# An encoder trunk on one core: activations stored by the parity of their tokens, and matmuls that read two runs in turn

## The chip, the core and the metric

The kernel runs on one core of one Trainium2 chip. The metric is device time in microseconds (us), the median of three runs. TensorE multiplies matrices: a block of 128 x 128 weights is loaded (the stationary operand), and then the columns of a moving operand are drawn through it and summed in PSUM. VectorE, ScalarE and the DMA queues prepare operands and take results away.

## What is computed

Two layers of an encoder on 256 tokens of width 2048. Each layer has a combined input projection, differential attention (8 heads) beside multi-head latent attention (8 heads), gated branches, an output projection, a SwiGLU block of width 5632, and a gated per-layer embedding:

```
h   = RMSNorm(x)
z   = h @ w_in[i]                  # diff q | k | v | q latent | kv latent | rope key | two gates
A   = differential attention;  B = multi-head latent attention
m   = sigmoid(gate_diff) * (A @ w_branch_diff) + sigmoid(gate_mla) * (B @ w_branch_mla)
x   = x + m @ w_out[i]
x   = x + SwiGLU(RMSNorm(x))
x   = x + sigmoid(RMSNorm(x) @ w_ple_gate) * (p[i] @ w_ple_in)
```

At the end stands one more RMSNorm. All inputs and outputs are float32. Attention is bidirectional, without a mask.

## The kernel before

Activations lie transposed: the 128 partitions hold features, the free dimension holds the 256 tokens (`T`). The stream `xT` has 16 such chunks. Every product keeps float32 accuracy by splitting both operands into a rounded part (`hi`, type float32r) and the remainder (`lo`), and summing three of the four partial products.

An operand tile is `[128, 512]`: columns 0 to 255 are `hi` of the 256 tokens, columns 256 to 511 are `lo`. The tiles `ua0` to `ua15` and `ub0` to `ub15` hold most operands; `fa`, `fb` and `fc` hold queries, keys and rotated queries. `split` fills a tile: ScalarE writes `hi` (L245, L246), VectorE the remainder (recorded under the helpers' lines L75 and L78).

The weights come by DMA in pieces of 512 KB (`piece`, tile `w`), and are split in the same way into `whi` (ScalarE, L182) and `wlo` (VectorE, L75).

`product` makes 128 output features for all tokens. For each of its chunks `emit` issues two matmuls:

- L212: weights `whi` against the whole operand tile, 512 columns (`hi` and `lo` side by side), into all 512 columns of an accumulator `mm`;
- L213: weights `wlo` against the `hi` half, 256 columns, into the second half of `mm`.

ScalarE and VectorE then add the two halves of `mm` (`joined`, or `accumulate` for the stream). The very last product of the program takes three matmuls of 256 columns instead (`whole`, L208 to L210).

`values` is the product with sides exchanged: the activations are stationary (128 tokens at a time), and the weights, 512 columns of `whi` or `wlo`, are the moving operand (L396 to L398). Its results `vals` have tokens in the partitions, as attention needs them. The host lays these weights out with `wide`, the others with `tiles`.

`scores` multiplies queries (stationary) by keys (moving, `three`). `turned` transposes the softmax weights on TensorE (L360), and the sums over keys follow (L568 for differential attention, L625 for latent attention). `norm` sums squares over partitions with a column of ones (L272), and `spread` turns the resulting two columns of 128 numbers into a row of 256 that stands in all partitions, with one matmul against a diagonal (L281). `rotated` exchanges halves of a head for the rotary embedding (L320). Those last ones, L568 too, are plain float32, which the program issues as two instructions each.

The order of instructions on each engine is set by a scheduler that simulates the program when it is built; DMA issues stand on SyncE's queue.

Of the kernel before, what the change touches and what calls it, by code (L numbers as in the profile page):

```python
# [19 lines left out]
P = 128  # L20
T = 256
# [32 lines left out]
def encoder(ctx, tc, x, p, positions, cols, lams, wq, wk, wv, wcq, wckv, wkr, wga, wgb,  # L54
            w_q_up, w_kn, w_v, w_bd, w_bm, w_out, w_gate, w_up, w_down, w_pin, w_pg, rope_c, out):
    nc = tc.nc
    V, A, PE = nc.vector, nc.scalar, nc.tensor
# [10 lines left out]
    def scratch(tag, bufs, n=T):  # L68
        return tmp.tile([P, n], F32, tag=tag, name=tag, bufs=bufs)

    def bank(ps=ps_at, tag="at", name="at", shape=(P, 2 * T)):
        return ps.tile(list(shape), F32, tag=tag, name=name)

    def tt(o, a, b, op):
        return V.tensor_tensor(out=o, in0=a, in1=b, op=op)  # L75

    def stt(o, a, s, b, op0, op1):
        return V.scalar_tensor_tensor(out=o, in0=a, scalar=s, in1=b, op0=op0, op1=op1)  # L78

    def ts(o, a, s1, s2, op0, op1=ALU.bypass):  # L80
        return V.tensor_scalar(out=o, in0=a, scalar1=s1, scalar2=s2, op0=op0, op1=op1)  # L81
# [10 lines left out]

    def operand(t):
        return t.rearrange("p c t -> p (c t)")


    xT = const.tile([P, NC, T], F32, name="xT")
# [15 lines left out]
    ones = const.tile([P, P], F32, name="ones")  # L113
# [81 lines left out]
    last_split, last_mm, chores, sq0, step = [], [], [], [], []  # L195
# [8 lines left out]
    def emit(acc, hi, lo, at, us, first, last, whole):  # L204
        for j, u in enumerate(us):
            s, start, stop = slice((at + j) * P, (at + j + 1) * P), first and j == 0, last and j == len(us) - 1
            if whole:
                PE.matmul(acc[:, :T], hi[:, s], u[:, :T], start=start, stop=False)  # L208
                PE.matmul(acc[:, :T], hi[:, s], u[:, T:], start=False, stop=False)
                PE.matmul(acc[:, :T], lo[:, s], u[:, :T], start=False, stop=stop)  # L210
            else:
                PE.matmul(acc, hi[:, s], u, start=start, stop=False)  # L212
                PE.matmul(acc[:, T:], lo[:, s], u[:, :T], start=False, stop=stop)  # L213

    def product(src, us, whole=False):

# [18 lines left out]
    def joined(acc, o=None):  # L235
        t = scratch("join", 3)
        A.activation(t, acc[:, T:], AF.Copy)  # L237
        o = scratch("a", 4) if o is None else o
        tt(o, acc[:, :T], t, ALU.add)
        return o  # L240

    def split(u, src, gain=None):
        hi, lo = u[:, :T], u[:, T:]
        if gain is None:
            return A.activation(hi, src, AF.Copy), tt(lo, src, hi.bitcast(F32), ALU.subtract)  # L245
        return A.activation(hi, src, AF.Copy, scale=gain), stt(lo, src, gain, hi.bitcast(F32), ALU.mult, ALU.subtract)  # L246

    def rsqrt(src, n, eps, width):

        v, y, a = (stat.tile([P, 2 * DH], F32, tag="r" + s, name="r" + s, bufs=2)[:, :width] for s in "vya")  # L250
        ts(v, src, 1.0 / n, eps, ALU.mult, ALU.add)
        ts(y.bitcast(I32), v.bitcast(I32), -0.5, 1597463007.0, ALU.mult, ALU.add)
        for _ in range(3):
            stt(a, y, -0.5, y, ALU.mult, ALU.mult)
            tt(a, a, v, ALU.mult)
            stt(y, a, 1.5, y, ALU.add, ALU.mult)
        return y
# [9 lines left out]
    def norm(sums, n):  # L267

        s = bank()
        for j, a in enumerate(sums):  # L270
            for b in range(2):
                PE.matmul(s[:, b : b + 1], a[:, b * P : (b + 1) * P], ones[:, 0:1], start=j + b == 0, stop=j + b == len(sums))  # L272
        return rsqrt(s[:, 0:2], n, EPS, 2)

    def spread(col, copied=True):

        dg = stat.tile([P, 2, P], F32, tag="dg", name="dg", bufs=1)
        for b in range(2):
            ts(dg[:, b, :], ident, col[:, b : b + 1], None, ALU.mult)
        s = bank()  # L280
        PE.matmul(s[:, :T], ones, dg, start=True, stop=True)  # L281
        if not copied:
            return s[:, :T]
        row = stat.tile([P, T], F32, tag="row", name="row", bufs=2)
        A.activation(row, s[:, :T], AF.Copy)  # L285
        return row
# [11 lines left out]
    def stream(us, gain):  # L298

        acc = squares()  # L300

        def add(c):
            split(us[c], xT[:, c, :], g(gain, c))
            square_into(acc, xT[:, c, :], c == 0)

        return acc, add
# [11 lines left out]
    def rotated(a, c_, s_, o=None):  # L318
        r = bank()
        PE.matmul(r[:, :T], swap, a, start=True, stop=True)  # L320
        t = scratch("sh", 2)
        tt(t, r[:, :T], s_, ALU.mult)
        tt(a, a, c_, ALU.mult)
        tt(a, a, t, ALU.add)
        if o is None:
            for j, t in enumerate(krs):
                split(t[64 * j : 64 * j + 64], a[64 * j : 64 * j + 64])
        else:
            split(o, a)

    def three(q, k):
        return [(q[:, :T], k[:, T:]), (q[:, T:], k[:, :T]), (q[:, :T], k[:, :T])]

    def scores(*maps):

# [41 lines left out]
    def values(src, us, load=None):  # L377

        vals = stat.tile([P, 2, 2, 512], F32, tag="vals", name="vals", bufs=1)
        n = len(us)  # L380
        order = [(half, a, 2) for half in range(2) for a in range(0, n, 2)]
        if load:
            order = [(half, a, 1) for a in range(BOTH) for half in range(2)] + [s for s in order if s[1] >= BOTH]
        banks = {}
        for half, a, m in order:
            if a == 0:
                banks[half] = [bank(ps_mm, "mm", "mmv") for _ in range(2)]
            if load and not half:
                load(a, m)
            hi, lo = piece(src[half][:, a * 512 : (a + m) * 512], 4 * m)  # L390
            for j in range(m):
                s = slice(j * 512, (j + 1) * 512)
                for b in range(2):
                    xh = us[a + j][:, b * P : (b + 1) * P]
                    xl = us[a + j][:, T + b * P : T + (b + 1) * P]
                    PE.matmul(banks[half][b], xh, hi[:, s], start=a + j == 0, stop=False)  # L396
                    PE.matmul(banks[half][b], xl, hi[:, s], start=False, stop=False)  # L397
                    last_mm[:] = [PE.matmul(banks[half][b], xh, lo[:, s], start=False, stop=a + j == n - 1)]  # L398
            if half or a + m < n:
                yield  # L400
            if a + m == n:
                for b in range(2):
                    A.activation(vals[:, b, half, :], banks[half][b], AF.Copy)
                if not half:
                    yield vals
# [15 lines left out]
    for L in range(DEPTH):  # L421
# [27 lines left out]


        qk = [(ub[h], operand(fa(h, F32R))) for h in range(DH)]

        def queries_keys(h):
            for which, w in enumerate((wq, wk)):
                a = joined(product(w[L, h], ua))
                sh = scratch("sh", 2)
                V.stream_shuffle(sh, a, ROPE16)
                tt(sh, sh, sr, ALU.mult)
                tt(a, a, cr, ALU.mult)
                tt(a, a, sh, ALU.add)  # L460
                split(qk[h][which], a)


        cq, ckv = ub[8:12], ub[12:14]
        qn, kn, qr = [], [], ub[14:]
# [19 lines left out]
        def queries_up(n):  # L485
            for acc in pair(w_q_up[L, n : n + 2], cq):
                if n < MH:
                    qn.append(operand(fa(len(qn), F32R)))
                    split(qn[-1], joined(acc))
                else:  # L490
                    if n > MH:
                        qr.append(operand(fc(len(qr) - 2, F32R)))
                    at = qr[len(qr) - 1] if n > MH else qr[ropes[0]]
                    rotated(joined(acc), cos_m, sin_m, at)
                    ropes[0] += 1
# [149 lines left out]
        acc, add = stream(ub, f"g_ffn{L}")  # L645
# [11 lines left out]
        for part, (f0, f1) in enumerate(FF_PARTS):  # L657
            for f in range(f0, f1):
                a = pre.pop(0) if pre else joined(product(w_gate[L, f], ub))
                tt(a, a, R, ALU.mult)  # L660
                s = scratch("sig", 2)
# [3 lines left out]
                b = pre.pop(0) if pre else joined(product(w_up[L, f], ub))  # L665
# [3 lines left out]
            if last:  # L669
                acc, add = stream(ub, f"g_ple{L}")  # L670
# [12 lines left out]
        if final:  # L683
            sums = [squares(), squares()]
# [5 lines left out]
        else:  # L690
            acc, add = stream(ua, f"g_mix{L + 1}")
        for n in range(NC):
            if final and n == NC - 1:
                a = scratch("a", 4)
                tt(a, product(w_pg[L, n], ub, True), R, ALU.mult)
            else:
                a = pre.pop(0) if pre else joined(product(w_pg[L, n], ub))
                tt(a, a, R, ALU.mult)
            s = scratch("sig", 2)
# [6 lines left out]
    for n, m in ((0, 1), (1, 1), (2, 2), (4, 4), (8, 4), (12, 4)):  # L706
        o = xT[:, n : n + m, :]
# [32 lines left out]
def wide(w):  # L740

    d, k, n = w.shape
    w = w.reshape(d, k // P, P, n // 512, 512).transpose(0, 3, 2, 1, 4)
    return np.ascontiguousarray(w).reshape(d, n // 512, P, k // P * 512)


# [47 lines left out]
```

## Time and profile before

| | before |
|---|---|
| median of three runs | 2865.66 us (2865.38 to 2865.86) |
| span of the profiled execution | 2863.7 us |
| TensorE matmul busy | 2846.3 us |
| VectorE busy | 2063.5 us |
| ScalarE busy | 1523.5 us |
| DMA queue of the weights | 529.01 MB, 56.4% of 16 engines |

The profiled execution's own time is its span, from the first to the last instruction, and what lies around it; the page gives the span alone, and the median of the runs stands 2.0 us above it. Matmuls are pipelined: the next one starts before the last has ended, so the durations of matmuls add up to more than the busy time, and the distance from one start to the next tells what a matmul takes of the engine. "PE" is TensorE's matmul, "PEld" its weight load. A row of the groups has the line, the engine and operation, the tile written and those read, the shapes, the count, then busy time in us and mean ns of one, then idle time ahead of it.

### The profile page before, as it was taken

What the parts mean: (1) busy time and instruction counts of PE and PEld (TensorE: products, weight loads), DVE (VectorE), ACT (ScalarE), POOL (GpSimd) and SP (SyncE); (2) the same over time, 40 slices, a digit from 0 to 9 for tenths busy, and PEclk for the clock granted to TensorE, in tenths of its full rate; (3) what the DMA queues carried; (4) which work ended last, traced back from release to release, by engine and by line L of the source; (5) the groups of instructions that cost most, each with busy time, mean ns of one, the idle gap of its engine ahead of it and who ended that gap; (6) DMA issues with size and microseconds to landing.
All of it is one profiled execution on the core that took longest, in us unless ns stands there. A gap on an engine that the chain in (4) does not pass through costs nothing.

```text
span 2863.7 us, 44001 instructions
## 1 busy us (share of the span) xinstructions
PE 2846.3 (99%) x16750; PEld 2507.5 (88%) x16750; DVE 2063.5 (72%) x3532; ACT 1523.5 (53%) x2532; POOL 1.7 (0%) x9
## 2 busy tenths in 40 slices
PE   9999999999999999999999999999999999999998
PEld 7888888888888888888888888888888888888887
DVE  7898658776666766677859976687766666666776
ACT  6676545554445444455646755555544444444554
POOL 0000000000000000000000000000000000000000
PEclk9999999999999999999999999999999999999999
DMA  7444455555565566566555444565556655655654
GB/s 240 165 167 150 160 194 197 195 189 189 184 198 194 186 197 198 195 194 192 186 190 166 152 155 169 193 199 193 190 187 186 197 196 186 201 195 194 192 191 140
DMA packets 156596, 532.41 MB, mean 186 GB/s; under 512 B 16992, under 2 KB 24160, under 8 KB 156384
## 3 DMA queue, kind: packets, MB, share of 16 engines
q1 hardware_dynamic: 155952, 529.01, 56.4%
q8 instruction: 131, 2.15, 0.3%
q14 instruction: 81, 0.66, 0.1%
q10 hardware_dynamic: 432, 0.59, 0.1%
HBM read 527.43 MB, written 2.10 MB: 185 GB/s over the span
## 4 chain that ended last, share of the span: by engine, by line
PE 98%; DVE 1%; ACT 0%; DMA 0%; issue 0%; SPq 0%; DVEq 0%; ACTq 0%
PE mm L212 61%; PE mm L213 31%; PE S L342 1%; PE mmv L398 1%; PE mmv L397 1%; PE mmv L396 1%; PE at L360 0%; PE at L568 0%; PE at L625 0%; DMA w<-in_wv 0%; DVE wlo L75 0%; DVE a L75 0%; PE at L281 0%; DVE xT L75 0%; ACT E L351 0%
## 5 line engine op out<-in xcount | busy, mean ns | idle before, releaser
L182 ACT ACTIVATE whi<-w 128x1024 fp32r<-128x1024 f32 (+2 forms) x1032 | 1067.3, 1034 | 1268.2 <-issue 722.8
L75 DVE TENSOR_TENSOR wlo<-w,whi 128x1024 fp32r<-128x1024 f32 (+2 forms) x1032 | 1229.6, 1191 | 699.9 <-ACT whi L182 690.8
L212 PE MATMUL mm<-ub,whi 128*128 128x512 f32 x3952 | 1360.9, 392 | 0.0
L212 PE MATMUL mm<-ua,whi 128*128 128x512 f32 x3744 | 1283.9, 390 | 0.0
L213 PE MATMUL mm<-ub,wlo 128*128 128x256 f32 x3952 | 1096.8, 278 | 0.0
L213 PE MATMUL mm<-ua,wlo 128*128 128x256 f32 x3744 | 1036.3, 277 | 0.0
L212 PEld LDWEIGHTS mm<-ub,whi 128*128 128x128 f32 x3952 | 741.9, 188 | 159.3
L212 PEld LDWEIGHTS mm<-ua,whi 128*128 128x128 f32 x3744 | 702.1, 188 | 143.9
L213 PEld LDWEIGHTS mm<-ub,wlo 128*128 128x128 f32 x3952 | 741.8, 188 | 0.8
L213 PEld LDWEIGHTS mm<-ua,wlo 128*128 128x128 f32 x3744 | 702.9, 188 | 2.3 <-DVE wlo L75 0.6
L75 DVE TENSOR_TENSOR a<-mm,join 128x256 f32<-128x256 f32 x421 | 175.4, 418 | 0.3 <-ACT join L237 0.2
L237 ACT ACTIVATE join<-mm 128x256 f32<-128x256 f32 x453 | 166.0, 367 | 5.1 <-PE mm L213 4.9
L75 DVE TENSOR_TENSOR xT<-xT,mm 128x256 f32<-128x256 f32 x256 | 106.8, 420 | 41.5 <-PE mm L213 37.7
L75 DVE TENSOR_TENSOR a<-a,row 128x256 f32<-128x256 f32 x207 | 87.3, 424 | 6.6 <-ACT row L285 0.8
L75 DVE TENSOR_TENSOR a<-a 128x256 f32<-128x256 f32 x120 | 51.1, 425 | 4.0
L396 PE MATMUL mmv<-whi,ua 128*128 128x512 f32 x128 | 50.4, 398 | 1.2 <-ACT whi L182 1.2
L75 DVE TENSOR_TENSOR ua<-a,ua 128x256 fp32r<-128x256 f32 x120 | 50.2, 418 | 1.0 <-ACT ua L245 1.0
L397 PE MATMUL mmv<-whi,ua 128*128 128x512 f32 x128 | 50.3, 397 | 0.0
L245 ACT ACTIVATE ua<-a 128x256 fp32r<-128x256 f32 x120 | 48.3, 403 | 2.6 <-DVE a L75 2.6
L351 ACT ACTIVATE E<-S,nm 128x256 f32<-128x256 f32 x96 | 44.2, 470 | 5.1 <-DVE nm L81 5.1
L398 PE MATMUL mmv<-wlo,ua 128*128 128x512 f32 x128 | 45.5, 397 | 0.1
L75 DVE TENSOR_TENSOR ssq<-ssq,sq 128x256 f32<-128x256 f32 x97 | 40.6, 419 | 0.5 <-ACT sq L264 0.5
(154 smaller groups left out, 1160.2 us busy)
## 6 DMA issues: line engine op xcount, KB each, us to landing
w<-in_w_gate SPq DMA_DIRECT2D x176, 512.0 KB, 4.6
w<-in_w_up SPq DMA_DIRECT2D x176, 512.0 KB, 4.6
w<-in_w_down SPq DMA_DIRECT2D x128, 512.0 KB, 4.3
w<-in_wga SPq DMA_DIRECT2D x64, 512.0 KB, 3.7
w<-in_wgb SPq DMA_DIRECT2D x64, 512.0 KB, 4.2
w<-in_w_out SPq DMA_DIRECT2D x64, 512.0 KB, 4.3
w<-in_w_pg SPq DMA_DIRECT2D x64, 512.0 KB, 4.4
w<-in_w_down SPq DMA_DIRECT2D x64, 384.0 KB, 3.6
```

Of the source, the lines that this page charges most:

```text
L75: return V.tensor_tensor(out=o, in0=a, in1=b, op=op)
L182: last_split[:] = A.activation(hi[:, :m], w[:, :m], AF.Copy), tt(lo[:, :m], w[:, :m], hi[:, :m].bitcast(F32), ALU.subtract)
L212: PE.matmul(acc, hi[:, s], u, start=start, stop=False)
L213: PE.matmul(acc[:, T:], lo[:, s], u[:, :T], start=False, stop=stop)
L237: A.activation(t, acc[:, T:], AF.Copy)
L245: return A.activation(hi, src, AF.Copy), tt(lo, src, hi.bitcast(F32), ALU.subtract)
L342: PE.matmul(S[:, b, :], q[:, b * P : (b + 1) * P], k, start=j == 0, stop=j == len(pairs) - 1)
L351: last_exp[0] = A.activation(E[:, b, :], S[:, b, :], AF.Exp, bias=nm[:, b : b + 1], scale=scale, accum_out=sm[:, b : b + 1])
L396: PE.matmul(banks[half][b], xh, hi[:, s], start=a + j == 0, stop=False)
L397: PE.matmul(banks[half][b], xl, hi[:, s], start=False, stop=False)
L398: last_mm[:] = [PE.matmul(banks[half][b], xh, lo[:, s], start=False, stop=a + j == n - 1)]
```

## The change

Operand tiles keep their 512 columns, in another order. The new order is parity first, then `hi` or `lo`, then the token: columns 0 to 127 hold `hi` of the even tokens, 128 to 255 `lo` of the even ones, 256 to 383 `hi` of the odd tokens, 384 to 511 `lo` of the odd ones. Two tokens that follow each other thus lie 256 words, 1,024 bytes, apart.

- `split` reads its source with a step of two words (`by_parity`) and writes two runs of 128 for `hi`, and two for `lo` (`parts`). Queries that serve as stationary operand keep the old order (`plain=True`).
- `emit` draws the moving operand in the order of the tokens (`in_turn`): column after column, in turn from the one and from the other run. The results in PSUM stand in the order of the tokens, as before.
- Where activations are stationary (`values`, `norm`), a block of 128 tokens is now the even or the odd ones, and so are the two blocks of keys in attention: `three` reads the keys as two runs of 128.
- `wide` on the host sorts the 512 columns of a block of the values' weights by parity, and `values` draws them in turn.
- `spread` draws the two halves of its diagonal in turn.

No instruction is added or removed, and on each engine they stand in the same order as before. Tiles keep their sizes and addresses.

```diff
+    def parts(u):
+        return u.rearrange("p (c h t) -> p h c t", c=2, h=2)
+
+    def in_turn(u):
+        return u.rearrange("p (c h t) -> p h t c", c=2, h=2)
+
+    def by_parity(row):
+        return row.rearrange("p (t c) -> p c t", c=2)
...
     def emit(acc, hi, lo, at, us, first, last, whole):
         for j, u in enumerate(us):
+            t = in_turn(u)
...
-                PE.matmul(acc, hi[:, s], u, start=start, stop=False)
-                PE.matmul(acc[:, T:], lo[:, s], u[:, :T], start=False, stop=stop)
+                PE.matmul(acc, hi[:, s], t, start=start, stop=False)
+                PE.matmul(acc[:, T:], lo[:, s], t[:, 0], start=False, stop=stop)
...
-    def split(u, src, gain=None):
-        hi, lo = u[:, :T], u[:, T:]
+    def split(u, src, gain=None, plain=False):
+        if plain:
+            hi, lo = u[:, :T], u[:, T:]
+        else:
+            src = by_parity(src)
+            hi, lo = (parts(u)[:, j] for j in range(2))
...
-                PE.matmul(s[:, b : b + 1], a[:, b * P : (b + 1) * P], ones[:, 0:1], start=j + b == 0, stop=j + b == len(sums))
+                PE.matmul(s[:, b : b + 1], by_parity(a)[:, b], ones[:, 0:1], start=j + b == 0, stop=j + b == len(sums))
...
-        PE.matmul(s[:, :T], ones, dg, start=True, stop=True)
+        PE.matmul(s[:, :T], ones, dg.rearrange("p b t -> p t b"), start=True, stop=True)
...
     def three(q, k):
-        return [(q[:, :T], k[:, T:]), (q[:, T:], k[:, :T]), (q[:, :T], k[:, :T])]
+        k = parts(k)
+        return [(q[:, :T], k[:, 1]), (q[:, T:], k[:, 0]), (q[:, :T], k[:, 0])]
...
-                    xh = us[a + j][:, b * P : (b + 1) * P]
-                    xl = us[a + j][:, T + b * P : T + (b + 1) * P]
-                    PE.matmul(banks[half][b], xh, hi[:, s], start=a + j == 0, stop=False)
-                    PE.matmul(banks[half][b], xl, hi[:, s], start=False, stop=False)
-                    last_mm[:] = [PE.matmul(banks[half][b], xh, lo[:, s], start=False, stop=a + j == n - 1)]
+                    xh, xl = (parts(us[a + j])[:, k, b] for k in range(2))
+                    wh, wl = (w[:, s].rearrange("p (c t) -> p t c", c=2) for w in (hi, lo))
+                    PE.matmul(banks[half][b], xh, wh, start=a + j == 0, stop=False)
+                    PE.matmul(banks[half][b], xl, wh, start=False, stop=False)
+                    last_mm[:] = [PE.matmul(banks[half][b], xh, wl, start=False, stop=a + j == n - 1)]
...
 def wide(w):
-    w = w.reshape(d, k // P, P, n // 512, 512).transpose(0, 3, 2, 1, 4)
+    w = w.reshape(d, k // P, P, n // 512, 256, 2).transpose(0, 3, 2, 1, 5, 4)
```

More of the change, by code (lines that the diff above doesn't have):

```diff
@@ L206, in emit @@
             s, start, stop = slice((at + j) * P, (at + j + 1) * P), first and j == 0, last and j == len(us) - 1
+            t = in_turn(u)
             if whole:
-                PE.matmul(acc[:, :T], hi[:, s], u[:, :T], start=start, stop=False)
-                PE.matmul(acc[:, :T], hi[:, s], u[:, T:], start=False, stop=False)
-                PE.matmul(acc[:, :T], lo[:, s], u[:, :T], start=False, stop=stop)
-            else:
-                PE.matmul(acc, hi[:, s], u, start=start, stop=False)
-                PE.matmul(acc[:, T:], lo[:, s], u[:, :T], start=False, stop=stop)
+                PE.matmul(acc[:, :T], hi[:, s], t[:, 0], start=start, stop=False)
+                PE.matmul(acc[:, :T], hi[:, s], t[:, 1], start=False, stop=False)
+                PE.matmul(acc[:, :T], lo[:, s], t[:, 0], start=False, stop=stop)
+            else:
+                PE.matmul(acc, hi[:, s], t, start=start, stop=False)
+                PE.matmul(acc[:, T:], lo[:, s], t[:, 0], start=False, stop=stop)
     def product(src, us, whole=False):
@@ L328, in rotated @@
         else:
-            split(o, a)
+            split(o, a, plain=True)
     def three(q, k):
-        return [(q[:, :T], k[:, T:]), (q[:, T:], k[:, :T]), (q[:, :T], k[:, :T])]
+        k = parts(k)
+        return [(q[:, :T], k[:, 1]), (q[:, T:], k[:, 0]), (q[:, :T], k[:, 0])]
     def scores(*maps):
@@ L460, in queries_keys @@
                 tt(a, a, sh, ALU.add)
-                split(qk[h][which], a)
+                split(qk[h][which], a, plain=which == 0)
         cq, ckv = ub[8:12], ub[12:14]
@@ L488, in queries_up @@
                     qn.append(operand(fa(len(qn), F32R)))
-                    split(qn[-1], joined(acc))
+                    split(qn[-1], joined(acc), plain=True)
                 else:
```

## The prediction

> **What bounds the kernel now.** I read the page from the top: shares of the engines, the 40 slices, the chain that ended last, the groups.
>
> ```profile
> PE 2846.3 (99%) x16750; PEld 2507.5 (88%) x16750; DVE 2063.5 (72%) x3532; ACT 1523.5 (53%) x2532; POOL 1.7 (0%) x9
> PEclk9999999999999999999999999999999999999999
> PE 98%; DVE 1%; ACT 0%; DMA 0%; issue 0%; SPq 0%; DVEq 0%; ACTq 0%
> L212 PE MATMUL mm<-ub,whi 128*128 128x512 f32 x3952 | 1360.9, 392 | 0.0
> L212 PE MATMUL mm<-ua,whi 128*128 128x512 f32 x3744 | 1283.9, 390 | 0.0
> L213 PE MATMUL mm<-ub,wlo 128*128 128x256 f32 x3952 | 1096.8, 278 | 0.0
> L213 PE MATMUL mm<-ua,wlo 128*128 128x256 f32 x3744 | 1036.3, 277 | 0.0
> ```
>
> TensorE is busy 2846.3 of 2863.7 us at full granted clock, 98% of the chain that sets the end lies on it, and its large groups show no idle time ahead of them. So the time is the sum of the start-to-start distances of its matmuls, and nearly all of that is 3952 + 3744 = 7,696 pairs: one matmul of 512 columns (L212), one of 256 (L213). The timeline of TensorE gives what a pair takes. Two stretches, 16 pairs from the first row to the last of each (every other row left out is an L213):
>
> ```profile
> 1000.25 0.39 PE L212 MATMUL mm<-ua,whi 128*128 128x512 f32 x1
> 1000.48 0.28 PE L213 MATMUL mm<-ua,wlo 128*128 128x256 f32 x1
> ...
> 1005.69 0.39 PE L212 MATMUL mm<-ua,whi 128*128 128x512 f32 x1
> ```
> ```profile
> 664.01 0.40 PE L212 MATMUL mm<-ub,whi 128*128 128x512 f32 x1
> 664.24 0.28 PE L213 MATMUL mm<-ub,wlo 128*128 128x256 f32 x1
> ...
> 669.61 0.40 PE L212 MATMUL mm<-ub,whi 128*128 128x512 f32 x1
> ```
>
> 5.44 us / 16 = 340 ns in the first, 5.60 / 16 = 350 ns in the second. The busy time by stretches, of line L212 alone (its count stands in brackets, the granted clock after the two engines), says that both paces last:
>
> ```profile
> core 0: us, PE busy (x) PEld busy (x), PEclk, DMA share, GB/s
> 634.00:770.00 136.00, 135.93 (x389) 72.94 (x389) 1.00 0.57 183
> 1366.00:1438.00 72.00, 61.90 (x177) 33.09 (x176) 1.00 0.57 187
> 2054.00:2190.00 136.00, 135.93 (x389) 72.95 (x389) 1.00 0.55 184
> 2786.00:2852.00 66.00, 56.32 (x161) 30.08 (x160) 0.99 0.40 136
> 900.00:1000.00 100.00, 100.00 (x296) 55.21 (x295) 1.00 0.59 186
> ```
>
> 136 us / 389 = 350 ns, 100 / 296 = 338 (one or two of the count reach over the ends). The same two instructions run at two paces under the same clock of 1.00. So it isn't the array's clock that sets a pair's length; something that feeds the array falls short, by an amount that differs from stretch to stretch.
>
> How short is read from matmuls that ask for less per unit of time. The float32 matmuls (L281, L320, L568) take about twice as long per column as the rounded ones (float32r, L212, L213), so they draw columns at half the pace:
>
> ```profile
> L281 PE MATMUL at<-dg,ones x22: 378/379/796, 61.4 to 2854.4; 128*128 128x256 f32 x22
> L320 PE MATMUL at<-a,rc x20: 377/379/483, 195.7 to 1651.8; 128*128 128x256 f32 x20
> L568 PE MATMUL at<-vals,wt x128: 270/275/275, 135.0 to 1653.6; 128*128 128x128 f32 x128
> 1353.57 0.59 PE L281 MATMUL at<-dg,ones 128*128 128x256 f32 x2
> 135.12 0.89 PE at L568 x8
> ```
>
> The first three rows give durations (least/median/most), the fourth is from the timeline, the last from the chain. The fourth holds two matmuls in 0.59 us of which the last lasts 0.379, so they start 0.21 us apart: 256 float32 columns occupy the engine for about 0.21, as 512 rounded ones should. I take 215 ns, with L320's like duration behind it. Against L212 that is 379 to 390 and 392 ns, 11 to 13 less; in the first stretch L213 follows L212 by 0.23, against 0.215 the same within the view's hundredths. I take 12. Eight L568 in 0.89 us are 111 ns each, each with a weight block of its own; against L213 it is 275 to 277 and 278, 2 to 3 less. **So a pair has about 12 + 2 = 14 ns of shortfall at the quick pace and 24 at the slow one.** It goes with the columns drawn, not with the instruction, and shows in the pair's quick drawing alone.
>
> [...]
>
> **The change, part by part.** (1) The moving operand of every product is drawn in turn from two runs 1,024 bytes apart, each column from the other run than the last. Each run then advances at half the pace, one column per two, which is the pace at which the float32 rows show no shortfall. No row of this trace has a moving operand that isn't contiguous, so the price is bounded: from below, each column can cost what the float32 rows allow, 215 ns per 512 and half of that, 107.5, per 256, a pair of 322.5; from above, a column drawn from a fresh place each time costs at least what a float32 column does, 215/256 = 0.84 ns, a pair of 645. I take 215 + 111 = 326, since the L568 rows, with a new weight block each, come no closer than 111. The pair's quick drawing is the one thing that separates L212 from those rows, and this edit eases that.
>
> Sum: 7,696 x 14 = 107.7 us. The four stretches at the slow pace hold 389 + 177 + 389 + 161 = 1,116 pairs, 10 ns more each: 11.2.
>
> (2) The values' products (L396 to L398) draw weights instead, and the host lays those out by parity.
>
> ```profile
> 1451.11 0.39 PE L396 MATMUL mmv<-whi,ua 128*128 128x512 f32 x1
> ...
> 1452.95 0.40 PE L398 MATMUL mmv<-wlo,ua 128*128 128x512 f32 x1
> ```
>
> Eight distances in 1.84 us, 230 ns each. Of L396 there are 128 + 16, of the other two lines as many:
>
> ```profile
> L396 PE MATMUL mmv<-whi,ua x128: 387/393/500, 4.5 to 1472.7; 128*128 128x512 f32 x128
> L396 PE MATMUL mmv<-whi,ub x16: 387/394/397, 227.9 to 1656.4; 128*128 128x512 f32 x16
> ```
>
> For 432 such matmuls: (230 - 215) x 432 is 6.5 us. The weights' DMAs keep number, size and queue, and the order of instructions on every engine stays as it is.
>
> (3) The 316 splits of activations (a ScalarE copy and a VectorE subtract each) read every second word and write two runs of 128. Nearest rows:
>
> ```profile
> L75 DVE TENSOR_TENSOR ua<-a,ua 128x256 fp32r<-128x256 f32 x120 | 50.2, 418 | 1.0 <-ACT ua L245 1.0
> L245 ACT ACTIVATE ua<-a 128x256 fp32r<-128x256 f32 x120 | 48.3, 403 | 2.6 <-DVE a L75 2.6
> L75 DVE TENSOR_TENSOR wt<-at,wt 128x512 fp32r<-128x512 f32 x16 | 10.9, 682 | 0.0
> L362 ACT ACTIVATE wt<-at 128x512 fp32r<-128x512 f32 x16 | 9.5, 594 | 5.3 <-PE at L360 5.3
> ```
>
> I cost them at nothing. If a step of two words cost as much as twice the words, VectorE would gain 316 x (682 - 418) = 83 us, (2063 + 83) / 2740 = 78% busy, still under TensorE; ScalarE 316 x (594 - 403) = 60 us, 58%. The products of the other tiles cover both. Where that cover is gone, at the last split ahead of a new stage, some ten places a layer would wait 0.3 us longer each, 6 us; I leave that to the range. Below nothing isn't to be had: the words are the same.
>
> (4) The stationary sides of the norms' few matmuls (L272) read with a step, and the spread (22, L281) draws its two halves in turn. Between no change and a doubling of 379 ns the 22 cost 0 to 8 us; I take nothing, as the float32 pace has slack. The scores read keys as two runs of 128: the columns stay consecutive, nothing.
>
> Total: 107.7 + 11.2 + 6.5 = 125.4 us. 2863.7 - 125.4 = 2738.3 of span; the median of the runs shown stands 2.0 us above the profiled span (2865.66), so 2740.
>
> **The rivals.** *Partial:* only the long matmul gains, 12 ns, because the short one is held by its weight load, and the two paces stay. 7,696 x 12 + 6.5 = 98.9 us, 2767. For it: L213 is within 2 to 3 ns of the weight-bound L568. It is the same sign and lies in the likeliest case's own range, 2712 (the pair at 322.5: 3.5 x 7,696 = 27 us more) to 2790.
>
> *Nothing:* the shortfall isn't in how the operand is read, but follows columns as such, say where the results are written, which the change leaves as consecutive as before. For it: one pace holds through changes of tile, ua or ub. Against: the float32 rows write as many results per column drawn, and the two paces need a cause that the writing, the same in both stretches, doesn't name. 2866, and within 0.2% (5.7 us, about what a measurement of this kernel can tell from no change).
>
> *Slower:* the feed fetches neighbouring words together and keeps only the last fetch, so that a column from the other run needs a fetch of its own. Place: every L212 and L213. It decides as soon as a column in turn costs over 340/768 = 0.443 ns, that is 0.02 more than the float32 rows' half, 0.42. Price: at 0.84 ns a column a pair takes 645, (645 - 340) x 7,696 = 2,347 us more, some 5,210 in all. For it: a contiguous read has its shortfall in proportion to the columns, as a fetch of a fixed number of words would. Against: nothing in the trace, which has no such read.
> [...]
>
> **How the numbers follow.** Full gain 0.55, partial 0.16, nothing 0.11, slower 0.18. [...] Predicted is the full gain, 2740. The range from 2700 to 2872 holds the first three and leaves out the slower case; below, it takes 10 us beyond the bound of 322.5 for stages whose pace I read too slow. Faster 0.71, same 0.11, slower 0.18.
>
> **What would show it.** Right: L212's mean near 379, L213's near 275, 16 pairs in 5.2 us, one pace in all stretches, TensorE still 98% or more, splits still covered. Partial: L212 shorter, L213 as before, pairs near 328. Nothing: 340 and 350 again. Slower: L212's duration over 600, weight loads at half their share. I would be wrong by a missed cover if VectorE's splits near 700 ns came with idle time of TensorE ahead of L212; and by the mechanism if the gain sat in the 256-column matmuls.

## The result and the profile after

The changed kernel takes 2751.22 us (median of 4 runs, 2751.01 to 2751.38) against 2865.76 before (of 4 as well, one more than in the table before): ratio 0.96, 95% interval 0.9587 to 0.9614, 114.5 us less. The profiled span is 2749.4 us.

The page after, first the shares and the chain, then the groups of the products (L222 is the matmul of 512 columns, L223 that of 256) and one pair of groups of the splits:

```profile
PE 2728.5 (99%) x16750; PEld 2499.9 (91%) x16750; DVE 2069.4 (75%) x3532; ACT 1546.5 (56%) x2532; POOL 1.7 (0%) x9
PE 97%; DVE 1%; ACT 1%; DMA 0%; issue 0%; SPq 0%; DVEq 0%; ACTq 0%
L222 PE MATMUL mm<-ub,whi 128*128 128x512 f32 x3952 | 1299.4, 383 | 0.9 <-DVE a L75 0.6
L222 PE MATMUL mm<-ua,whi 128*128 128x512 f32 x3744 | 1234.3, 383 | 0.0
L223 PE MATMUL mm<-ub,wlo 128*128 128x256 f32 x3952 | 1077.3, 273 | 0.0
L223 PE MATMUL mm<-ua,wlo 128*128 128x256 f32 x3744 | 1022.1, 273 | 1.5 <-DVE wlo L75 1.5
L259 ACT ACTIVATE ua<-a 128x256 fp32r<-128x256 f32 x120 | 59.1, 493 | 2.6 <-DVE a L75 2.6
L75 DVE TENSOR_TENSOR ua<-a,ua 128x256 fp32r<-128x256 f32 x120 | 54.9, 457 | 1.2 <-ACT ua L259 1.2
```

TensorE still sets the time. Its long matmul went from 390 and 392 ns to 383, the short one from 277 and 278 to 273. The splits became longer (ScalarE 403 to 493, VectorE 418 to 457), off the path.

TensorE's timeline, 16 pairs from the first row to the last:

```profile
960.16 0.38 PE L222 MATMUL mm<-ua,whi 128*128 128x512 f32 x1
960.38 0.27 PE L223 MATMUL mm<-ua,wlo 128*128 128x256 f32 x1
...
965.40 0.38 PE L222 MATMUL mm<-ua,whi 128*128 128x512 f32 x1
```

5.24 us / 16 = 327.5 ns a pair, where before had 340 and 350. Busy time by stretches, L222 alone, first the place that ran at the slow pace before, then one that ran at the quick pace:

```profile
core 0: us, PE busy (x) PEld busy (x), PEclk, DMA share, GB/s
612.00:740.00 128.00, 127.94 (x391) 73.67 (x392) 1.00 0.61 196
866.00:962.00 96.00, 96.00 (x294) 55.38 (x293) 1.00 0.61 192
```

128 / 391 = 327 and 96 / 294 = 327: one pace is left.

### The profile page after: what moved, and what is told of

The parts are those of the page before. It is cut to its first block, busy times and chain, and to the rows that moved or that the text cites. A ratio compares the mean times of both kernels' runs of the same rounds, so it can differ in the third digit from the quotient of the medians.

```text
span 2749.4 us, 43991 instructions
## 1 busy us (share of the span) xinstructions
PE 2728.5 (99%) x16750; PEld 2499.9 (91%) x16750; DVE 2069.4 (75%) x3532; ACT 1546.5 (56%) x2532; POOL 1.7 (0%) x9
## 4 chain that ended last, share of the span: by engine, by line
PE 97%; DVE 1%; ACT 1%; DMA 0%; issue 0%; SPq 0%; DVEq 0%; ACTq 0%
PE mm L222 60%; PE mm L223 30%; PE S L357 1%; PE mmv L411 1%; PE mmv L413 1%; PE mmv L412 1%; PE at L375 0%; PE at L583 0%; PE at L640 0%; DVE wlo L75 0%; ACT whi L191 0%; DMA xT<-in_x 0%; ACT E L366 0%; DVE a L75 0%; PE at L295 0%
## 5 line engine op out<-in xcount | busy, mean ns | idle before, releaser
L222 PE MATMUL mm<-ub,whi 128*128 128x512 f32 x3952 | 1299.4, 383 | 0.9 <-DVE a L75 0.6
L222 PE MATMUL mm<-ua,whi 128*128 128x512 f32 x3744 | 1234.3, 383 | 0.0
L223 PE MATMUL mm<-ub,wlo 128*128 128x256 f32 x3952 | 1077.3, 273 | 0.0
L223 PE MATMUL mm<-ua,wlo 128*128 128x256 f32 x3744 | 1022.1, 273 | 1.5 <-DVE wlo L75 1.5
L222 PEld LDWEIGHTS mm<-ub,whi 128*128 128x128 f32 x3952 | 746.5, 189 | 106.1 <-DVE a L75 1.7
L222 PEld LDWEIGHTS mm<-ua,whi 128*128 128x128 f32 x3744 | 706.8, 189 | 96.3
L223 PEld LDWEIGHTS mm<-ub,wlo 128*128 128x128 f32 x3952 | 758.7, 192 | 0.9
L223 PEld LDWEIGHTS mm<-ua,wlo 128*128 128x128 f32 x3744 | 718.6, 192 | 4.4 <-DVE wlo L75 2.7
L259 ACT ACTIVATE ua<-a 128x256 fp32r<-128x256 f32 x120 | 59.1, 493 | 2.6 <-DVE a L75 2.6
```

What stands on the lines that cost most here:

```text
L222: PE.matmul(acc, hi[:, s], t, start=start, stop=False)
L223: PE.matmul(acc[:, T:], lo[:, s], t[:, 0], start=False, stop=stop)
```

## The experiments

Ten kernels. Those that change an order of drawing alone, without the storage that belongs to it, work on permuted, repeated or other numbers; their instructions keep shapes and counts. "In turn" means that the columns come alternately from two runs, "in order" that they come one after the other as they are stored. A pair's time runs from the start of its long matmul to the start of the next long one.

### The order of drawing, undone piece by piece

`e1_in_order`, an edit of the changed kernel:

```diff
-            t = in_turn(u)
+            t = u.rearrange("p (h t) -> p h t", h=2)
```

> The changed kernel, but the products draw their operand tiles in the order in which they are stored, all 512 (or the first 256) columns one after the other; the sums then stand in the order of storage, so what follows works on permuted numbers. Splits, values, norms and spreads stay as changed. If the gain comes from the order in which TensorE draws the operand (my theory), L222 and L223 go back to 340 to 350 ns a pair and the time to 2751 + 7,696 x (343 - 328) = about 2866, less the few us of the values: 2855 to 2862. If it comes from where the operands lie in memory (runs of 128 written apart), the time stays at 2751.

Measured: 2849.59 us, ratio to before 0.9944 (0.9929 to 0.9959). The groups of its products:

```profile
L222 PE MATMUL mm<-ub,whi 128*128 128x512 f32 x3952 | 1349.8, 390 | 0.0
L223 PE MATMUL mm<-ub,wlo 128*128 128x256 f32 x3952 | 1091.7, 276 | 0.0
```

390 and 276, as before, with operands stored as changed. The order of drawing in the products is worth 2849.59 - 2751.22 = 98.4 us, 12.8 ns a pair. What the kernel still gains over before, 16.2 us, is accounted for by two other parts of the change, which below gain 5.9 (e10) and 11.4 us (e6) when each is put into the kernel before; so the place of the numbers shows no gain of its own. The time came out 5 us under what I expected, since nearly all pairs ran at 340: by the starts in the trace, 322 of its 7,545 whole pairs stood at 350 or 351 ns, against 1,463 before. Another part of the change had taken most of the slow pace away.

`e2_values_in_order`, an edit of the changed kernel:

```diff
-                    wh, wl = (w[:, s].rearrange("p (c t) -> p t c", c=2) for w in (hi, lo))
+                    wh, wl = (w[:, s] for w in (hi, lo))
```

> The changed kernel, but the values' products (L411 to L413) draw their weights one column after the other, so the values' features stand in another order than the reference's. Theory that the order of drawing is what counts: 432 matmuls go from 216 back to 230 to 236 ns, plus 6 to 9 us, 2757 to 2760. Rival, that the values waited for their weights anyway: 2751 within 2 us.

Measured: 2757.57 us, ratio 0.9623 (0.9607 to 0.9639): 6.35 us more than the changed kernel, on the lower edge of what I expected.

`e10_values_alone` puts that part alone into the kernel before (with `wide` on the host as changed):

```diff
+                wh, wl = (w[:, s].rearrange("p (c t) -> p t c", c=2) for w in (hi, lo))
...
-                    PE.matmul(banks[half][b], xh, hi[:, s], start=a + j == 0, stop=False)
+                    PE.matmul(banks[half][b], xh, wh, start=a + j == 0, stop=False)
```

> The kernel before with one part of the change alone: the values' weights sorted by parity on the host and drawn in turn. 432 matmuls from 235 to 216 ns: minus 8 us by the distances in the trace, minus 6.4 by the difference that undoing it made in the changed kernel, 2857 to 2859; the products keep both paces.

Measured: 2860.0 us, ratio 0.9979 (0.9969 to 0.9989), 5.9 us less than before, a microsecond less gain than I expected. One of its ten executions took 13,091 us, which I can't explain; the others lie from 2858.73 to 2861.31. The products kept both paces, and 1,574 pairs stood at 350 or 351 ns, 111 more than before: at 10 ns each, that is the missing microsecond.

`e3_short_in_order`, an edit of the changed kernel:

```diff
-                PE.matmul(acc[:, T:], lo[:, s], t[:, 0], start=False, stop=stop)
+                PE.matmul(acc[:, T:], lo[:, s], u[:, :T], start=False, stop=stop)
```

> The changed kernel, but the matmul of 256 columns (L223) draws the first 256 columns of the tile in order; the one of 512 in turn as changed. My prediction's step (the short one is held by its weight load at 111 and gains 2 ns): plus 15 us, 2766. What the profile after suggests (114.7 to 109.6, the short one falls short in proportion to its columns like the long one): plus 7,696 x 4 to 5 = 31 to 39 us, 2782 to 2790.

Measured: 2791.87 us, ratio 0.9742 (0.9728 to 0.9757), 40.7 us more than the changed kernel. So the short matmul isn't held by its weight load, as I had thought; its order of drawing counts too.

```profile
L222 PE MATMUL mm<-ub,whi 128*128 128x512 f32 x3952 | 1320.0, 378 | 0.5 <-DVE a L75 0.5
L223 PE MATMUL mm<-ub,wlo 128*128 128x256 f32 x3952 | 1102.0, 279 | 0.0
```

With one of the two in order, the long one falls to 378 and the short one rises to 279. By the starts in the trace (means, pairs with a stop of over 400 ns left out) the pair is 332.9 ns, 5.4 more than the 327.5 with both in turn. By the medians the long one takes 215 where it took 218 with both in turn, and the short one 118 where it took 109. 118 is what the short one took at the slow pace before; at the quick pace it took 113. So the two matmuls influence each other, and the 40.7 us are not simply the short one's part of the gain.

### What the slow pace hung on

`e6_spread_in_turn`, one edit of the kernel before:

```diff
-        PE.matmul(s[:, :T], ones, dg, start=True, stop=True)
+        PE.matmul(s[:, :T], ones, dg.rearrange("p b t -> p t b"), start=True, stop=True)
```

> The kernel before with one part of the change alone: spread draws its diagonal in turn (its row of factors then has another order than the tokens). The first four runs left open why the slow pace of 350 ns is nearly gone even where the products draw in order again. If the pace is set by how the matmuls ahead of a stretch end, and the spread is what stands there: the stretches at 350 ns shrink from 1,460 pairs to about 330, and the time to 2866 - 11 = 2855. If it is the norms' weight blocks or the values that set it: 2866 within 3 us.

Measured: 2854.01 us, ratio 0.9959 (0.9945 to 0.9973), 11.4 us less than before. Busy time of L212 in a stretch that ran at 350 before:

```profile
634.00:770.00 136.00, 135.93 (x401) 74.98 (x401) 1.00 0.60 188
```

401 matmuls where there were 389: 339 ns a pair. Eleven spreads in the whole program, drawn in another order, move about a sixth of all pairs from 350 to 340: 155 are left at 350 or 351, of 1,463, fewer than the 330 that I expected. How the spread does that, no run shows.

`e9_spread_in_order` takes the same edit out of the changed kernel.

> The changed kernel with spread drawing its diagonal in order again, so that its row of factors stands in another order than the tokens. Open: whether products drawn in turn still have two paces. If a drawing that is never short has one pace whatever stands ahead of it: 327.5 ns a pair throughout and 2751 within 2 us. If the slow pace comes back with the spread's order, at a sixth of the pairs: up to 2751 + 11 = 2762.

Measured: 2750.35 us, ratio 0.9597 (0.9582 to 0.9611), 0.9 us less than the changed kernel, which the two intervals don't separate. The same row of its stretches:

```profile
612.00:740.00 128.00, 127.89 (x392) 73.79 (x391) 1.00 0.60 195
```

Products drawn in turn have one pace with the spread in either order. The 0.9 us is near what the spread itself pays for being drawn in turn: its 22 matmuls last 434 ns in the changed kernel and 380 here (medians; 22 x 54 = 1.2 us).

```profile
L295 PE MATMUL at<-dg,ones x22: 431/434/794, 58.7 to 2740.0; 128*128 128x256 f32 x22
L295 PE MATMUL at<-dg,ones x22: 379/380/797, 58.9 to 2739.2; 128*128 128x256 f32 x22
```

The first row is of the changed kernel, the second of e9. By the starts, too, the first of a spread's two matmuls is followed by the second after 269 ns in turn and 219 in order (medians). So to draw in turn isn't quick for every operand: this one, plain float32 at half the columns per unit of time (219 ns for its 256 in order, where the short matmul of the products takes 109 in turn), became slower by it.

### Which orders are quick, and why

`e4_distances` and `e5_patterns` give each stage of the SwiGLU block an order of its own, each by lines like these:

```diff
+            elif mode[0] == "d4":
+                PE.matmul(acc, hi[:, s], u.rearrange("p (g c t) -> p g t c", c=2, t=4), start=start, stop=False)
+                PE.matmul(acc[:, T:], lo[:, s], u[:, :T].rearrange("p (g c t) -> p g t c", c=2, t=4), start=False, stop=stop)
```

> Stages of the SwiGLU block draw in different orders, each on a line of its own; the results are permuted numbers. d128, d64, d32, d16, d8, d4: columns in turn from two runs 128, 64, ... 4 words apart (512 down to 16 bytes). d2: two words apart inside four. step2: every second word. four: four runs of 128 in turn. plain: in order. narrow_plain and narrow_turn: in order and in turn, with weight blocks of 64 columns instead of 128 in all but the first and last chunk. Theory A, pace (each run advances at half pace, wherever it lies): 328 ns a pair for all distances from d128 to d8, four no slower, step2 as slow as plain or slower. [...] Theory D, collision with the weight load: narrow_plain, with half as much weight to load, falls from 340 to about 334, or to 328; with the feed alone at fault it stays at 340.

> Orders of drawing in the SwiGLU block again, each on its own line, results are permuted or repeated numbers. [...] t2, t4, t8, t16: two, four, eight or sixteen words of one run, then as many of the other. twice: each word drawn twice, one run at half pace. four_times: each word four times. turn_s2, turn_s4: in turn, every second or fourth word of each run. step4: every fourth word of one run. [...]

Their whole times (2873.35 and 3133.43, one profiled execution each) mix all orders. The long matmul's groups, of e4 first (L237 d4, L243 step2, L222 d128, L246 four, L240 d2, L249 plain, L252 narrow_plain, L255 narrow_turn):

```profile
L237 PE MATMUL mm<-ub,whi 128*128 128x512 f32 x512 | 167.7, 382 | 0.0
L243 PE MATMUL mm<-ua,whi 128*128 128x512 f32 x256 | 161.1, 629 | 0.0
L222 PE MATMUL mm<-ub,whi 128*128 128x512 f32 x416 | 136.6, 383 | 0.0
L246 PE MATMUL mm<-ua,whi 128*128 128x512 f32 x256 | 107.4, 445 | 0.0
L240 PE MATMUL mm<-ua,whi 128*128 128x512 f32 x256 | 87.1, 389 | 0.0
L249 PE MATMUL mm<-ua,whi 128*128 128x512 f32 x224 | 76.2, 389 | 0.0
L252 PE MATMUL mm<-ua,whi 128*64 128x512 f32 x192 | 66.4, 389 | 0.0
L255 PE MATMUL mm<-ua,whi 128*64 128x512 f32 x192 | 63.3, 379 | 0.0
```

And of e5 (L237 turn_s4, L222 t2, L234 turn_s2, L240 step4, L231 t16, L243 four_near, L246 plain, L225 t4, L249 twice):

```profile
L237 PE MATMUL mm<-ub,whi 128*128 128x512 f32 x416 | 269.1, 647 | 0.0
L222 PE MATMUL mm<-ub,whi 128*128 128x512 f32 x416 | 205.9, 508 | 0.0
L234 PE MATMUL mm<-ub,whi 128*128 128x512 f32 x512 | 174.2, 389 | 0.0
L240 PE MATMUL mm<-ua,whi 128*128 128x512 f32 x256 | 163.7, 640 | 0.0
L231 PE MATMUL mm<-ub,whi 128*128 128x512 f32 x448 | 161.3, 403 | 0.0
L243 PE MATMUL mm<-ua,whi 128*128 128x512 f32 x224 | 90.3, 435 | 0.0
L246 PE MATMUL mm<-ua,whi 128*128 128x512 f32 x256 | 89.6, 395 | 0.0
L225 PE MATMUL mm<-ua,whi 128*128 128x512 f32 x224 | 84.3, 417 | 0.0
L249 PE MATMUL mm<-ua,whi 128*128 128x512 f32 x256 | 83.9, 382 | 0.0
```

The mean distance from one pair's start to the next, from the starts in the trace, with the words that the first columns draw:

| order | words drawn | running in one group of four | ns a pair |
|---|---|---|---|
| plain | 0 1 2 3 4 5 | 2 | 340.6 (e4), 350.0 (e5) |
| d2 | 0 2 1 3 4 6 | 2 | 340.2 |
| turn_s2 | 0 256 2 258 4 260 | 2 | 340.1 |
| step2 | 0 2 4 6 8 10 | 1 | 680.3 |
| step4 | 0 4 8 12 16 20 | 1 | 693.3 |
| turn_s4 | 0 256 4 260 8 264 | 1 | 680.6 |
| d4 | 0 4 1 5 2 6 | 4 | 327.5 |
| d8 to d128 | 0 8 1 9 ..., 0 128 1 129 | 4 | 327.5 to 328.1 |
| twice | 0 0 1 1 2 2 | 4 | 327.5 |
| four_times | 0 0 0 0 1 1 | 8 | 327.5 |
| t2, t4, t8, t16 | 0 1 256 257 2 3 (t2) | back and forth | 494.9, 376.9, 366.7, 360.0 |
| four, four_near | 0 128 256 384 1; 0 4 8 12 1 | back and forth | 419.9, 404.2 |

What follows. Distance plays no part from 16 bytes (d4, 327.5) to 1,024 (the changed kernel, 327.5), so a cause that hangs on how far apart the two runs lie, anywhere between these, is out. Half pace of a run, the reason that my prediction gave, isn't enough: t2 draws each run at half pace too, and takes 494.9; four draws each run at a quarter, and takes 419.9.

The column "running in one group of four" takes every other column drawn, and counts how many of these, one after the other, come from one group of four neighbouring words (0 to 3, 4 to 7 and so on). In the steady orders, those above "back and forth" in the table, the time goes with this count: 680.3 to 693.3 for one, 340.1 to 350.0 for two, 327.5 to 328.1 for four and 327.5 for eight. From one to two it halves (680.3 to 340.2), from two to four it falls by 12.5 ns (340 to 327.5), and eight bring nothing more. I made this count after seeing these numbers, no run tests it by itself, and no trace shows what in TensorE stands behind it. It doesn't order those that go back and forth between the runs: t2, four and four_near have a count of one and take less than 680, and t4, t8 and t16 have a count of two, as plain does, and take more than 340. It doesn't tell why the spread became slower in turn (219 to 269 ns from the first of its matmuls to the second). Nor does it tell where the second pace of the plain order comes from: e5's plain stage ran at 350 although its spread was drawn in turn, so more than the spread sets that pace. In e5 that stage follows t8, in e4, where plain ran at 340.6, it follows d128; no run changes that alone.

Narrow weight blocks (64 columns) leave the plain order at its 340 (341.3 on the mean), so the shortfall doesn't hang on how much weight is loaded (theory D). In turn they give 325.0 (216.0 + 109.0 by the starts). With full blocks 2.5 ns a pair remain, 19 us in 7,696 pairs.

`e7_step16` and `e8_step64` ask whether those 2.5 ns hang on addresses:

```diff
-STEP = 48
+STEP = 16
```

> The changed kernel with the pad between the tiles of wlo and whi at 16 words in place of 48, so that whi and all tiles behind it lie 128 bytes lower. Open: the 2.5 ns by which a pair with full weight blocks (327.5) stands over one with half blocks (325.0). If that is the weight load touching the same part of memory as the drawing, other addresses of whi change it by some ns a pair, 2751 plus or minus 8 to 20 us; if it is a fixed cost of a longer weight load, 2751 within 2 us.

> The same with 64 words, whi 64 bytes higher than in the changed kernel. By addresses: another change than with 16 words, 2751 plus or minus 8 to 20 us. By a fixed cost: 2751 within 2 us.

Measured: 2751.68 us, ratio 0.9603 (0.9584 to 0.9622), and 2750.98, ratio 0.96 (0.9581 to 0.9619), both within 0.5 us of the changed kernel. It doesn't hang on these addresses, as a fixed cost wouldn't; what of a full block causes it stays open. No experiment pointed to a version that is clearly quicker than the changed one: e9 gains 0.9 us, and its output is permuted.

## Why the prediction was right, point by point

- **What bounds the kernel.** Right: TensorE, before and after, and by how its operand is drawn, not by its clock, which was granted at 0.998 before and after. e1 shows it: the order of drawing alone brings 98.4 of the 114.5 us.
- **Per pair, 12 + 2 = 14 ns.** That the shortfall lies in the drawing was right, the term a little too large: 340 to 327.5 is 12.5, and 98.4 us stand where 107.7 were forecast. Within it the parts were mis-sized against each other. The long matmul gained 8 to 9 (by the starts in the trace, medians 227 to 218), not 12, and the short one 4 (113 to 109), not 2. So about a third of the pair's gain sat in the matmul of 256 columns; that the gain sat there was the prediction's own sign against its mechanism. The mean durations became 383 and 273, where it gave 379 and 275. The step that failed is the weight bound taken from L568's 111 ns: the distance behind L223 is now 109, so 111 was no bound for it, and e3 cost 40.7 us where that step gave 15.
- **The slow stretches, 11.2 us.** They vanish, as forecast, but that the size is near is in part luck. I had counted 1,116 slow pairs in four windows; the trace has 1,463, which at 10 ns each are 14.6 us. And there are two ways to the same gain. Products drawn in turn have no slow pace (e9), and the spread's new order alone takes most of it away (e6, 11.4 us: 1,308 pairs at 10 ns, less some 1.2 that the spread itself pays). I had costed the spread at nothing, since its float32 pace would have slack; it had none (380 to 434 ns). As either edit does it, the gains don't add, and no run shows this term by itself in the changed kernel: 98.4 + 6.35 by undoing leave 9.8 of the 114.5 us.
- **The values, 6.5 us.** Right: 6.35 (e2) and 5.9 (e10, with a microsecond lost to more slow pairs).
- **The splits, nothing.** Right in the main: VectorE gained 2069.4 - 2063.5 = 6 us and ScalarE 23, where the bounds were 83 and 60 (for 316 splits; by the shapes in the trace after, 300 read and write in the new order), and the products cover them. TensorE's time not busy rose from 2863.7 - 2846.3 = 17.4 us to 20.9, by less than the 6 us that I left to the range. Two waits that TensorE has after, the second of which it didn't have before (line, what it waited for, us in total, times, longest):

```profile
PE mmv L411 <- ACT whi L191: 1.9, 2, 1.6
PE mm L223 <- DVE wlo L75: 1.5, 4, 0.5
```

- **The reason.** Not borne out. Columns drawn in turn from two runs are quick, but half pace by itself isn't why (t2). The rows of float32 matmuls, from which I argued, gave nearly the right pair (326 for 327.5); why they do stays open, and such a matmul itself became slower when it was drawn in turn (the spread). What makes an order quick is shown by e4 and e5 order by order, and not as a mechanism.
- **The rivals.** "Partial" is out by its mechanism, since the short matmul gained (2751 against 2767), and the long one alone in turn gives 2792 (e3). (The likeliest case's lower end comes to 2713 by its own sum, not 2712.) "Nothing" is out. "Slower" is out too (0.96). Its reason, a fetch for each column, no run shows, but a wrong order does cost as much as it gave: step2 took 680 ns a pair, close to the 645 that I worked out. It would have come true with every second word of one run (step2), with every fourth of two runs in turn (turn_s4, 680.6), or in part with two words at a time (t2, 495).

Sum: 114.5 us measured, 125.4 forecast. Of the difference, 9.3 us are the pair (98.4 for 107.7), and 1.4 the slow stretches, whose 9.8 is what the other two leave. A sum of three runs that were measured apart, 98.4 (e1), 11.4 (e6) and 5.9 (e10), is 115.7, 1.2 more than the whole.

## What to carry to other kernels

Where TensorE is never idle, compare the distance from start to start of its matmuls with that of matmuls which draw more slowly: a shortfall can lie in how the moving operand is drawn, as here (340 ns a pair, where I worked out 326 from the slower rows), and drawing the same operand in another order tells. For the float32r operands of these products, an order that takes even columns from one run of four words and odd ones from another, each run to its end, cut the pair from 340 to 327.5, at distances from 16 to 1,024 bytes. A plain float32 operand lost by it (the spread, 380 to 434 ns). A nearby order can cost double (step2, 680.3), so measure orders as stages of one kernel, each on a line of its own, before building the storage for one.

## What the runs showed that I had not expected

- The distance between the two runs doesn't matter: 327.5 to 328.1 ns a pair from 16 bytes to 512, and 327.5 at the changed kernel's 1,024.
- A step of two words costs double the plain order, 680 against 340 ns a pair; drawing a word two or four times costs no more than drawing in turn, 327.5.
- Eleven spreads' order of drawing sets the pace of some 1,300 pairs, when these draw in a plain order: 350 or 340 ns, 11.4 us in all.
- A plain float32 operand drawn in turn is slower: 434 against 380 ns for each of the spread's matmuls.
- A full weight block costs 2.5 ns a pair over a half one when the columns are drawn in turn (327.5 against 325.0).
